# Four of the long-convolution filters' pieces move ahead of the first block's attention

## The chip, the core and the metric

The kernel runs on one core of one Trainium2 chip. The metric is the device time of one execution in microseconds (us). The core has a matrix engine (TensorE, PE in the profile, with its weight loads as PEld), a vector engine (VectorE, DVE), an activation engine (ScalarE, ACT), a general engine (GpSimd, POOL) and SyncE (SP), whose queue issues most of the transfers.

## The reference, cut to what matters

Two kinds of layers follow each other, two of each; the change stands in the first kind (`first_block`), so it acts twice. A layer of it takes x of 512 positions by 1024 channels and computes, in float32:

```
h = rms_norm(x, pre_norm[l])
q, k, v, z_a, u_h, z_h, g_a, g_h = split(h @ w_in[l])
o = diff_attention(q, k, v, lam, rel_bias)       # 4 heads, 4 blocks of 128 queries
y_a = rms_norm(o, subln[l]) * (1 - lam_init) * silu(z_a)
filt = hyena_filters(...)                        # needs no x at all
z = fft_long_conv(hv, filt[:, 0], ...) * hx1
z = fft_long_conv(z, filt[:, 1], ...) * hx2
y_h = z * silu(z_h)
x = x + rms_norm((sigmoid(g_a) * (y_a @ w_pa) + sigmoid(g_h) * (y_h @ w_ph)) @ w_out)
```

`hyena_filters` is a small network of three sine layers over 512 positions, then one product with `w_out` for 2 directions, 2 orders and 512 channels, a decay `exp(-t * |delta|)`, and a transform to frequencies. Attention has two softmaxes for each head; the second is subtracted, scaled by `lam`.

## The kernel before

Large products are made of three float32r matmuls each (`mm3`, L258 to L260), on weights and activations split into a high and a low part (`split`: L266 makes the high part on ACT, L267 the low part on DVE, or on POOL for every third weight chunk). A projection of 128 columns takes 24 such matmuls of 512 columns (`projT`), on one weight chunk that is loaded (L280) and split first.

`layer1` opens the filters as a generator, `filters(l)`, and runs it in pieces, each to its next `yield`. Three pieces are the sine layers (matmul L467; the vector chain L469 to L478; the sine L479). After them come four groups, one for each of 2 orders and 2 halves of the channels, and a group has six pieces:

- four pieces t = 0 to 3, each with four matmuls (L503, L504) on the sines' result `a3` (L482, L483), the decay's exponent on ACT (L508 to L511), the product with it on DVE (L512), and a sum and a difference on POOL (L514, L515). Pieces 0 and 1 split their result (L266, L267), piece 3 makes two more combinations on POOL (L522, L524) and splits both. The first of the four also loads and splits the group's weights (L492, L493, L266, L267 as `fwh` and `fwl`) and its `deltas` (L496, L497).
- two pieces of transform, with twelve matmuls each (`mm3` in `bank`), DVE work L542 to L554, POOL L555, and in the second piece four stores to DRAM (L556, L557).

The pieces use tiles of tag `f`, of which there are eight in turn, and two banks of accumulators that are the filters' alone in this stage (`fl`, `ft`).

Three pieces run before the values' projection. The other 24 are drawn inside `attention1`, one or two ahead of each block of queries:

```
NX, ZS, FS = (1, 1, 1, 0), (3, 3, 7, 11, 13, 14, 15), (2, 1, 2, 1)
for _ in proj(-1):            # keys and queries of head 0
    pass
for hd in range(4):
    for i in range(4):
        for _ in range(FS[i]):
            next(flt, None)   # pieces of the filters
        # scores L667, L668; bias and maximum L671; L675
        # exponentials L677; L680 to L684; next(nxt): projections
```

`FS` says how many pieces go ahead of blocks 0 to 3 of a head, `NX` how many steps of the next head's projections go behind a block, `ZS` when the convolution's own projections (`hyena_v`) are drawn. The bias of a head has one buffer, loaded at the head's start (L449).

This is the order of the program. The order on each engine is another: the kernel is built in `tile.TileContext(nc, schedule_with_timeline_sim=True)`, so a planner with a time model puts the instructions into each engine's list, taking at each moment, among those whose inputs it believes ready, the one that stands earliest in the program. On the chip each engine then works its list in that order.

Of the kernel before, what the change touches and what calls it, by code (L numbers as in the profile page):

```python
# [168 lines left out]
class Kern:  # L169
# [390 lines left out]
    def attention1(self, l, h, v, flt, zv):  # L560
# [31 lines left out]
        def proj(hd):  # L592

            if hd < 3:
                ps = self.ps("acc")
                self.projT(self.wchunk(A[f"win{l}"][5 + hd], 8, P), h, ps)

                ka, kb = (self.T("qk", dt=F32R) for _ in range(2))
                la, lb = rest[hd % 2]
                nc.scalar.activation(ka[a], ps[a], AF.Copy)  # L600
                nc.scalar.activation(kb[b], ps[b], AF.Copy)
                nc.vector.tensor_tensor(la[a], ps[a], ka[a].bitcast(F32), op=SUB)
                nc.vector.tensor_tensor(lb[b], ps[b], kb[b].bitcast(F32), op=SUB)
                nc.gpsimd.tensor_copy(ka[b], ka[a])
                nc.gpsimd.tensor_copy(kb[a], kb[b])
                yield
                ps = self.ps("acc")
                self.projT(self.wchunk(A[f"win{l}"][1 + hd], 8, P), h, ps)

                qa, qb = (self.T("qk", dt=F32R) for _ in range(2))  # L610
                nc.scalar.activation(qa[a], ps[a], AF.Copy, scale=0.125)
                nc.scalar.activation(qb[b], ps[b], AF.Copy, scale=0.125)
                stt(qa[b], ps[a], 0.125, qa[a].bitcast(F32), op0=MUL, op1=SUB)
                stt(qb[a], ps[b], 0.125, qb[b].bitcast(F32), op0=MUL, op1=SUB)
                qk[hd + 1] = (qa, ka, la), (qb, kb, lb)
                yield
            if hd >= 0:
                ps = self.ps("acc")
                self.projT(self.wchunk(A[f"win{l}"][12 + hd], 8, P), h, ps)
                gate[hd] = self.T("o")  # L620
                self.silu2(gate[hd], ps)
# [25 lines left out]
            nc.gpsimd.memset(la[b].bitcast(F32), 0.0)  # L647
            nc.gpsimd.memset(lb[a].bitcast(F32), 0.0)

        NX, ZS, FS = (1, 1, 1, 0), (3, 3, 7, 11, 13, 14, 15), (2, 1, 2, 1)  # L650
        for _ in proj(-1):
            pass
        for hd in range(4):
# [199 lines left out]
    def layer1(self, l, h):  # L853
        nc, A = self.nc, self.A
        self.c1 = self.cq.tile([P, C1_N], F32, tag=f"c1{l}", name=f"c1{l}")
        nc.sync.dma_start(self.c1, A[f"c1{l}"])

        with self.stage(f"a{l}", dict(v=1, p=4, wt=2, o=4)):
            with self.stage(f"q{l}", dict(qk=8, ql=2, bias=1)), self.stage(f"f{l}", dict(f=8, fw1=1, fw23=1, fb=1, a3=1, fd=1, fwh=1, fwl=1)):

                self.fx = self.X((P, 4, S), F32R)
                flt = self.filters(l)
                self.apart = True
                for _ in range(3):
                    next(flt)
                v = self.T("v", (P, 4, S))
                self.projN(v, [A[f"wv{l}"][kc] for kc in range(4)], h, S)
                if l == 0:
                    self.bias_table()
                ma = []  # L870
                ya = self.attention1(l, h, v, flt, self.hyena_v(l, h, ma))
                assert next(flt, 0) == 0
                self.apart = False
        if "ya" in self.dbg:
            self.dump(ya, "ya")
        with self.stage(f"b{l}", dict(mg=1)):
            mg = []
            with self.stage(f"h{l}", dict(Y=4, iv=1, hx=2, gz=1, e=2, y=1)), \
                    self.stage(f"i{l}", dict(sd=2, sds=1, qd=4, hs=4, w=4, ab=2)):
                z = self.hyena(l, h, self.gates(l, h, ma, mg))  # L880
            self.mix1(l, h, ya, z, ma, mg)
# [778 lines left out]
```

## Time and profile before

| | |
|---|---|
| three runs | 1885.38, 1890.8, 1893.59 us; median 1890.8 |
| profiled execution, its own time | 1893.08 us |
| its span, first to last instruction | 1891.3 us |
| mean granted TensorE clock | 0.992 of full |
| PE busy | 98% of the span |
| DVE, ACT, POOL busy | 66%, 48%, 35% |

A matmul's end in the profile is modelled, so a busy PE may still be waiting a little; idle time of an engine that sets no end costs nothing. The attention of the first layer of this kind lies at about 60 to 218 us of the span, that of the second at about 514 to 668 us.

### The profile page before, as it was taken

How to read it: one execution, taken by the hardware profiler on the slowest of the kernel's cores; microseconds unless marked ns; L12 is line 12 of the kernel's file. 1: busy time of each engine (PE TensorE's matmuls, PEld its weight loads, DVE VectorE, ACT ScalarE, POOL GpSimd, SP SyncE). 2: the span in 40 equal slices, each digit the busy share in tenths (PEclk: the TensorE clock that was granted, in tenths of full speed). 3: DMA queues.
4: the chain of work that ended last, by engine and by line, in shares of the span. 5: the costliest groups of instructions: out<-in, count | busy, mean ns of one | idle time of the engine just before them, and what ended most of it. 6: DMA issues, size and time to landing. Idle time of an engine off the chain costs nothing.

```text
span 1891.3 us, 26054 instructions
## 1 busy us (share of the span) xinstructions
PE 1854.0 (98%) x9604; PEld 1560.9 (83%) x9604; DVE 1254.6 (66%) x2238; ACT 900.1 (48%) x1761; POOL 659.9 (35%) x566
## 2 busy tenths in 40 slices
PE   8999999999999999999999999999999999999998
PEld 5878888887788788888888888888888888888886
DVE  6898688664788849775567954757235895465722
ACT  4766432334476542223455356656325535665631
POOL 2455343443245535443146332111114643311110
PEclk9999999999999999999999989999999998999999
DMA  5333433324323353233332321213343222121242
GB/s 178 98 120 110 145 112 107 112 89 164 116 96 106 105 160 108 100 101 123 128 105 70 97 73 30 69 59 115 101 136 101 79 84 79 36 69 59 77 131 90
DMA packets 75656, 190.84 MB, mean 101 GB/s; under 512 B 15714, under 2 KB 25698, under 8 KB 75528
## 3 DMA queue, kind: packets, MB, share of 16 engines
q1 hardware_dynamic: 69448, 184.71, 30.1%
q0 software_dynamic: 1696, 3.41, 0.7%
q10 hardware_dynamic: 4384, 1.05, 0.3%
q8 instruction: 76, 1.25, 0.3%
q14 instruction: 52, 0.43, 0.1%
HBM read 171.29 MB, written 17.84 MB: 100 GB/s over the span
## 4 chain that ended last, share of the span: by engine, by line
PE 75%; DVE 13%; issue 4%; ACT 3%; POOL 3%; DMA 2%; ACTq 0%; SPq 0%; DVEq 0%; POOLq 0%
PE acc L258 13%; PE acc L260 13%; PE acc L259 13%; PE fl L259 5%; PE fl L258 5%; PE fl L260 5%; PE av L1181 2%; DVE wl L267 2%; DVE g L1005 1%; PE av L259 1%; PE av L258 1%; PE av L260 1%; PE av L588 1%; PE lg L259 1%; PE lg L260 1%
## 5 line engine op out<-in xcount | busy, mean ns | idle before, releaser
L266 ACT ACTIVATE wh<-wr 128x1024 fp32r<-128x1024 f32 (+3 forms) x268 | 256.0, 955 | 448.3 <-PE acc L259 160.9
L258 PE MATMUL acc<-u,wh 128*128 128x512 f32 x996 | 397.1, 399 | 0.2
L259 PE MATMUL acc<-u,wh 128*128 128x512 f32 x996 | 393.2, 395 | 0.0
L260 PE MATMUL acc<-u,wl 128*128 128x512 f32 x996 | 392.5, 394 | 0.0
L267 POOL TENSOR_TENSOR wl<-wr,wh 128x1024 fp32r<-128x1024 f32 (+3 forms) x86 | 186.2, 2165 | 490.1 <-ACT wh L266 451.0
L267 DVE TENSOR_TENSOR wl<-wr,wh 128x1024 fp32r<-128x1024 f32 (+3 forms) x182 | 217.5, 1195 | 170.0 <-ACT wh L266 159.6
L258 PEld LDWEIGHTS acc<-u,wh 128*128 128x128 f32 x996 | 187.2, 188 | 42.7 <-issue 3.7
L260 PEld LDWEIGHTS acc<-u,wl 128*128 128x128 f32 x996 | 187.2, 188 | 39.5 <-issue 2.6
L259 PEld LDWEIGHTS acc<-u,wh 128*128 128x128 f32 x996 | 187.3, 188 | 38.3 <-issue 2.9
L259 PE MATMUL fl<-u,wh 128*128 128x512 f32 x316 | 128.6, 407 | 0.0
L260 PE MATMUL fl<-u,wl 128*128 128x512 f32 x316 | 126.5, 400 | 0.0
L258 PE MATMUL fl<-u,wh 128*128 128x512 f32 x316 | 125.9, 398 | 0.0
L260 PE MATMUL acc<-wh,u 128*128 128x512 f32 (+1 forms) x212 | 79.5, 375 | 0.3
L258 PE MATMUL acc<-wh,u 128*128 128x512 f32 (+1 forms) x212 | 78.2, 376 | 1.6 <-DVE l L702 1.2
L259 PE MATMUL acc<-wl,u 128*128 128x512 f32 (+1 forms) x212 | 78.7, 371 | 0.0
L260 PEld LDWEIGHTS fl<-u,wl 128*128 128x128 f32 x316 | 60.3, 191 | 14.9 <-issue 3.0
L259 PEld LDWEIGHTS fl<-u,wh 128*128 128x128 f32 x316 | 60.3, 191 | 13.3 <-issue 2.0
L258 PEld LDWEIGHTS fl<-u,wh 128*128 128x128 f32 x316 | 60.1, 190 | 13.2 <-issue 1.5
L677 ACT ACTIVATE p<-p,mx 128x512 f32<-128x512 f32 x64 | 45.7, 715 | 37.4 <-DVE mx L675 37.4
L790 POOL TENSOR_TENSOR w<-w,ab 128x256 f32<-128x256 f32 x32 | 37.7, 1179 | 69.2 <-DVE w L789 64.0
L321 ACT ACTIVATE sq<-x 128x512 f32<-128x512 f32 x40 | 25.2, 631 | 68.6 <-DVE x L1613 38.2
L1168 ACT ACTIVATE p<-p,amx 128x128 f32<-128x128 f32 (+1 forms) x64 | 35.8, 560 | 28.2 <-DVE amx L1167 27.5
(636 smaller groups left out, 4438.7 us busy)
## 6 DMA issues: line engine op xcount, KB each, us to landing
wr<-in_win SPq DMA_DIRECT2D x88, 512.0 KB, 3.5
wr<-in_xin SPq DMA_DIRECT2D x64, 512.0 KB, 3.4
wr<-in_xout SPq DMA_DIRECT2D x32, 512.0 KB, 3.5
hd<-f SPq DMA_DIRECT2D x32, 256.0 KB, 4.2
hs<-hd SPq DMA_DIRECT2D x32, 256.0 KB, 2.8
wr<-in_wout SPq DMA_DIRECT2D x16, 512.0 KB, 3.4
xd<-x SPq DMA_DIRECT2D x12, 512.0 KB, 3.1
x<-xd SPq DMA_DIRECT2D x12, 512.0 KB, 4.8
```

Source lines behind the costliest of these rows:

```text
L258: mm(ps, l[0], r[0], start=first, stop=False)
L259: mm(ps, l[0], r[1], start=False, stop=False)
L260: return mm(ps, l[1], r[0], start=False, stop=last)
L266: nc.scalar.activation(hi, src, AF.Copy)
L267: (nc.gpsimd if pool else nc.vector).tensor_tensor(lo, src, hi.bitcast(F32), op=SUB)
L321: self.nc.scalar.activation(self.T("sq"), self.xt(i)[:, h * S:(h + 1) * S], AF.Square, scale=1.0 / math.sqrt(D), accum_out=self.ms2[i][:, ...
L588: nc.tensor.matmul(po[:, i], wt[:, kt], v[:, kt, hd * P:(hd + 1) * P], start=kt == 0, stop=kt == 3)
L677: nc.scalar.activation(pp[c], pp[c], AF.Exp, bias=mx[:, c:c + 1], accum_out=s0[:, i:i + 1] if c == 0 else s)
L790: nc.gpsimd.tensor_tensor(a[:, 0], a[:, 0], b[:, 1], op=ADD)
L1005: nc.vector.scalar_tensor_tensor(y[:, d:], ps[:, :S - d], w(n), y[:, d:], op0=MUL, op1=ADD)
L1168: nc.scalar.activation(p[:, :n], p[:, :n], AF.Exp, bias=mx, scale=scale, accum_out=s)
L1181: mm(po[:, ts], v[hd // 4][:, k, (hd % 4) * P:(hd % 4 + 1) * P], w[:, k], start=k == 0, stop=k == i)
```

## The change

Four pieces are drawn between the values' projection (and, in the first layer, the bias table) and the attention; `FS` is lowered by one, so that 5 pieces stand beside each of the four heads and the sum stays 4 + 4 x 5 = 24. No instruction is added or taken away.

```
-        NX, ZS, FS = (1, 1, 1, 0), (3, 3, 7, 11, 13, 14, 15), (2, 1, 2, 1)
+        NX, ZS, FS = (1, 1, 1, 0), (3, 3, 7, 11, 13, 14, 15), (2, 1, 1, 1)
...
                 self.projN(v, [A[f"wv{l}"][kc] for kc in range(4)], h, S)
                 if l == 0:
                     self.bias_table()
+                for _ in range(4):
+                    next(flt)
                 ma = []
                 ya = self.attention1(l, h, v, flt, self.hyena_v(l, h, ma))
```

The four are pieces t = 0 to 3 of the first group. Before, a head held just one group; after, each head begins one piece further back in the cycle: head 0 has both transform pieces of group 0 ahead of its block 0 and then t = 0, 1, 2 of group 1, and so on, until head 3 ends on the last transform piece, as before.

## Rows read from the trace of the kernel before

**Rows 1.** The page: span, and busy time of each engine.
```profile
span 1891.3 us, 26054 instructions
...
PE 1854.0 (98%) x9604; PEld 1560.9 (83%) x9604; DVE 1254.6 (66%) x2238; ACT 900.1 (48%) x1761; POOL 659.9 (35%) x566
```

**Rows 2.** The page: the chain that ended last, by engine.
```profile
PE 75%; DVE 13%; issue 4%; ACT 3%; POOL 3%; DMA 2%; ACTq 0%; SPq 0%; DVEq 0%; POOLq 0%
```

**Rows 3.** Windows: stretch, length; busy PE, PEld, DVE, ACT, POOL; clock; DMA.
```profile
60.00:94.00 34.00, 34.00 (x184) 29.27 (x183) 30.48 (x57) 23.70 (x44) 14.60 (x13) 1.00 0.27 85
94.00:130.00 36.00, 34.11 (x181) 27.20 (x180) 32.97 (x57) 22.10 (x48) 20.05 (x17) 1.00 0.33 112
...
168.00:218.00 50.00, 50.00 (x279) 43.18 (x278) 43.89 (x81) 28.64 (x59) 21.87 (x20) 1.00 0.52 168
218.00:240.00 22.00, 22.00 (x111) 18.54 (x110) 5.01 (x8) 8.56 (x18) 4.72 (x3) 1.00 0.29 93
...
584.00:626.00 42.00, 39.88 (x216) 34.19 (x216) 36.73 (x60) 26.00 (x52) 24.01 (x19) 1.00 0.28 89
626.00:668.00 42.00, 39.01 (x226) 33.34 (x225) 32.64 (x68) 26.60 (x58) 23.86 (x19) 1.00 0.40 129
```

**Rows 4.** Waits of PE, 42 to 240 us: total, times, longest.
```profile
PE fl L258 <- DVE f L512: 1.1, 1, 1.1
PE tr L584 <- DVE o L640: 0.4, 1, 0.4
PE fl L503 <- DVE f L512: 0.3, 1, 0.3
PE fl L504 <- DVE fwl L267: 0.3, 1, 0.3
PE ft L503 <- DVE f L512: 0.2, 1, 0.2
```

**Rows 5.** Waits of PE, 500 to 700 us, the longest of them.
```profile
PE lg L667 <- DVE mx L671: 5.1, 3, 2.1
```

**Rows 6.** Timeline of DVE at a head's start in the second layer.
```profile
631.44 0.69 DVE L671 CUSTOM_DVE_ANT_0 p<-lg,bias 128x512 f32<-128x512 f32 x1 [1.52 <-DMA bias<-db]
```

**Rows 7.** Timeline of DVE: third sine's start and `a3`'s end, both layers.
```profile
52.36 0.80 DVE L469 TENSOR_SCALAR f<-ft,fb 64x512 f32<-64x512 f32 x1 [0.73 <-PE ft L467]
...
60.27 0.68 DVE L483 TENSOR_TENSOR a<-f,a 64x512 fp32r<-64x512 f32 x1 [0.81 <-ACT a L482]
...
513.61 0.80 DVE L469 TENSOR_SCALAR f<-fl,fb 64x512 f32<-64x512 f32 x1 [0.75 <-PE fl L467]
...
530.36 0.69 DVE L483 TENSOR_TENSOR a<-f,a 64x512 fp32r<-64x512 f32 x1
```

**Rows 8.** Timeline of PE: first score and first piece, in both layers.
```profile
60.12 0.39 PE L667 MATMUL lg<-qk,qk 128*128 128x512 f32 x1
...
65.11 0.28 PE L503 MATMUL fl<-fwh,a 128*128 128x256 f32 x1
...
514.30 0.39 PE L667 MATMUL lg<-qk,qk 128*128 128x512 f32 x1
...
531.72 0.28 PE L503 MATMUL ft<-fwh,a 128*128 128x256 f32 x1
```

**Rows 9.** Timeline of SP's queue: load of the first group's weights.
```profile
50.74 0.58 SPq L492 DMA_DIRECT2D f<-in_fwo  x1
```

**Rows 10.** Groups by line and form, DVE, 60 to 240 us.
```profile
L267 DVE TENSOR_TENSOR u<-f,u 128x512 fp32r<-128x512 f32 x16 | 12.3, 778 | 0.7 <-ACT u L266 0.7
...
L512 DVE TENSOR_TENSOR f<-fl,f 128x512 f32<-128x512 f32 x8 | 5.5, 685 | 0.1
...
L267 DVE TENSOR_TENSOR fwl<-f,fwh 128x512 fp32r<-128x512 f32 x3 | 3.1, 1041 | 0.1
```

**Rows 11.** Timeline of POOL and of DVE around 77 us.
```profile
76.99 1.30 POOL L522 TENSOR_TENSOR f<-x 128x512 f32<-128x512 f32 x1
...
77.09 1.74 DVE L684 SCALAR_TENSOR_TENSOR p<-p,cc,p 128x512 f32<-128x512 f32 x1
```

More of the change, by code (lines that the diff above doesn't have):

```diff
@@ L648, in attention1 @@
             nc.gpsimd.memset(lb[a].bitcast(F32), 0.0)
-        NX, ZS, FS = (1, 1, 1, 0), (3, 3, 7, 11, 13, 14, 15), (2, 1, 2, 1)
+        NX, ZS, FS = (1, 1, 1, 0), (3, 3, 7, 11, 13, 14, 15), (2, 1, 1, 1)
         for _ in proj(-1):
@@ L869, in layer1 @@
                     self.bias_table()
+                for _ in range(4):
+                    next(flt)
                 ma = []
```

## The prediction

> **What bounds the kernel now.** I read the page first: PE is busy for 98% of a span of 1891.3 us, DVE for 66%, the others for less [rows 1]. The chain that ended last is 75% PE and 13% DVE [rows 2]. So time is won only where PE stands still, and lost only where it is made to. The question is where PE stands still in the two stretches of attention, since the change moves work only there. The windows say it by head [rows 3]: in the first layer PE is busy for all of 34.00 us of head 0 and all of 50.00 us of head 3, and short by 36.00 - 34.11 = 1.9 us in head 1; in the second layer it is short by 2.1 us in 584 to 626 and by 3.0 in 626 to 668. DVE is close behind in the same stretches: 30.48 of 34, 32.97 of 36, 36.73 of 42 [rows 3]. The granted clock is 1.00 in all of them, the upper of its two levels (2.4 GHz), so no stretch has a slow clock to win back.
>
> Then PE's own waits. In the first layer they sum to 1.1 + 0.4 + 0.3 + 0.3 + 0.2 = 2.3 us, and 1.9 of these are waits for pieces of the filters (L512, and `fwl`) [rows 4]. In the second layer nearly all is one kind: a score (L667) that waits until DVE has taken the scores before it out of their bank (L671), 5.1 us in three waits [rows 5]. One of the three is not DVE's load: DVE itself stood for 1.52 us until the head's bias had landed in its one buffer [rows 6]. That leaves at least 5.1 - 1.5 = 3.6 us that come from DVE's being late. What the change could take away is thus 1.9 + 3.6 = 5.5 us, and all of PE's waits here are 2.3 + 5.1 = 7.4 us.
>
> **The change, part by part.** No instruction is added or removed: the 24 pieces, their loads and their stores all stay, so busy time on every engine stays, and what counts is when.
>
> *When the four can start.* In the program they now stand ahead of head 0's keys and queries, but they need `a3`, the last step of the third sine. In the first layer `a3` is ready at 60.27 + 0.68 = 60.95 us, in the second at 530.36 + 0.69 = 531.05 [rows 7]. The first scores start at 60.12 and at 514.30, the first piece's matmul at 65.11 and at 531.72 [rows 8]. This is the point of the argument: pieces 0 and 1 stood ahead of block 0's scores in the program before as well, and yet PE ran scores first, by 5.0 us in one layer and by 17.4 in the other. Readiness placed them, not the program. Moved up further, they still can't start before `a3`: 60.95 against 65.11 leaves at most 4.2 us, 531.05 against 531.72 leaves 0.7. The sines aren't moved. So the four pieces do not go into the projection ahead of attention, where DVE has room; they go closer together at the start of head 0, and pieces 2 and 3 go ahead of the softmax of blocks 1 and 2.
>
> *Their loads.* The first group's weights are loaded at 50.74 us [rows 9], 10 us before `a3`; earlier than that is worth nothing. Their place on SP's queue moves past the loads for keys and queries of head 0 and the bias. Should the load stand before one of those and wait for its `f` tile, the weight chunks behind it would be late; I cost this at nothing, since two chunks are loaded ahead and PE's 34.00 of 34.00 shows none late [rows 3]. If that cover were gone, a late chunk would cost up to the 1.5 us that the late bias cost DVE [rows 6].
>
> *What heads gain.* The four pieces are four products at 685 ns, four low parts at 778 and one `fwl` at 1041 on DVE [rows 10]: 4 x 0.685 + 4 x 0.778 + 1.04 = 6.9 us in a layer. A head held one whole group; heads 1 to 3 now hold a piece less, on the average 6.9 / 4 = 1.7 us of DVE less beside 36 to 50 us. That is the relief: from 92% of a head to about 87% (32.97 - 1.7 of 36). The waits worth 5.5 us are those where DVE is a little late, by 2.1 us at most [rows 5], so a relief of that size should remove some. Ends: nothing, if the planner fills the room with other work; all 5.5, if each wait is of that kind. I take about half, 3 us: the relief is as large as a typical wait, but it doesn't fall on the very block that is late.
>
> *What head 0 pays.* Four pieces follow each other at `a3`, on two banks, and then both transform pieces stand ahead of block 0 in the program. Ends: nothing, since head 0 lost nothing with three pieces in its first two blocks (34.00 of 34.00); or, in each layer, the 1.9 us that head 1 of the first layer loses with a group beside it [rows 3], 3.8 in all. I take 1 us, nearer to head 0's row, since it is the same head, and PE has other projections in reach there. What covers the delay of block 0's softmax is those projections; at the end of attention PE is still full, 22.00 of 22.00 with DVE at 5.01 [rows 3], so the store of such work does not run out.
>
> *Sum.* -3 + 1 = -2 us. The profiled execution took 1893.08 us, its span and 1.8 around it, so 1893.1 - 2 = 1891.1; it lies 2.3 above the runs' median of 1890.8, so on the median's scale 1888.8, say 1889. The bounds of the two terms, -5.5 and +3.8, give 1885 to 1895.
>
> **The rivals.**
>
> *Slower: PE waits in its list.* PE works its list in order. If the planner, believing `a3` earlier than it is, puts the first piece's matmul directly behind head 0's queries, PE stands until `a3`. In the first layer that is from 60.12 to 61.6 (`a3` and the 0.7 us that lay between it and L503 in the second layer), 1.5 us. In the second it is from 514.30: if the third sine then took the first layer's 8.6 us (52.36 to 60.95 [rows 7]), `a3` would be ready at 522.2, and PE would stand for 8.6 us; with its present 17.4 us, for 17. Together 10 to 19 us: 1901 to 1910. It decides from a place about 9 us too early in the second layer. For it: 531.72 is only 0.7 us behind `a3`, so the list there has no slack. Against it: the planner already had these pieces ahead in the program and did not do it. Chance 0.12.
>
> *Slower: POOL's sums hold DVE.* Beside a sum on POOL of 1.30 us (L522) a DVE product that started 0.10 us later took 1.74 us [rows 11]; its own end came 0.54 us after POOL's. The four pieces have ten such sums in a layer; if each came to hold the softmax's DVE work of head 0 by as much as 1.3 us, that is 13 us of DVE in a layer, and if half of it in both layers reached PE, 13 us: 1904. Against it: the same sums hold DVE somewhere today. Chance 0.06. The Trainium skill has the rule, on its page "SBUF — State Buffer", section "SBUF: two separate sides": VectorE and GpSimd have one pair of ports in common, and whoever starts first keeps it for its whole instruction. The trace agrees with that here, the 1.74 us above.
>
> *Faster: DVE paces the heads.* With DVE at 92% of head 1, the heads might shrink by all of DVE's relief: 6.9 us in each layer, 13.8 in all, 1877. Against it: the four pieces stay in head 0 by `a3`, and all of PE's waits in both stretches are 7.4 us; more than that can come only from later stages whose order falls better. Chance 0.18.
>
> *Nothing moves.* The lists come out nearly as before, since readiness rules: 1891. Chance 0.14.
>
> **How the numbers follow.** My forecast has 0.50. A measurement of this kernel tells about 0.5% from no change, 9.5 us: 1881.3 to 1900.3. Forecast and "nothing moves", 0.64, lie within. The faster rival, and a few cases of the forecast in which later stages gain too, make 0.20; the two slower ones, less the mildest of them, 0.16. The range reaches from 1878, which takes in most of the way to the faster rival's 1877, to 1902, which takes in the near end of the first slower one; the likeliest case alone is 1885 to 1895.
>
> **What would show it.** Right: the first L503 still starts behind the first scores and within some us of `a3`; L503 of pieces 2 and 3 closer behind, transform matmuls beside block 0 or 1; windows of heads 1 to 3 with DVE busy lower by some 1.7 us each, and PE's waits for L671 and L512 down from 7 to about 4 us. Wrong: a PE wait of several us at L503 just behind the first scores; `a3` itself ready earlier (the sines moved after all); or a difference that arises outside both stretches of attention.

## The result, and the profile after

The changed kernel is slower: median 1904.14 us of 8 runs (1898.87 to 1910.95) against 1890.89 us of 8 runs of the kernel before (1881.45 to 1894.87), ratio 1.0074, 95% interval 1.0054 to 1.0095. The forecast was 1889 us, its range 1878 to 1902. The profiled execution took 1898.87 us, the shortest of the eight. Its page, span, busy time and the chain that ended last, which answer to [rows 1, 2]:

```profile
span 1897.1 us, 26030 instructions
...
PE 1852.9 (98%) x9604; PEld 1561.6 (82%) x9604; DVE 1249.7 (66%) x2238; ACT 899.0 (47%) x1761; POOL 659.0 (35%) x566
...
PE 66%; DVE 15%; issue 3%; ACT 2%; POOL 2%; DMA 2%; ACTq 0%; SPq 0%; DVEq 0%; POOLq 0%
```

The work is the same to a few us, and each engine's count of instructions is the same; PE's part of the chain fell from 75% to 66%. The windows say in which heads (columns as in [rows 3]; the second layer now runs some 9 us later, so its two stretches are shifted by that):

```profile
60.00:94.00 34.00, 34.00 (x184) 29.24 (x183) 30.01 (x57) 23.43 (x44) 14.58 (x13) 1.00 0.27 85
94.00:130.00 36.00, 33.61 (x178) 28.59 (x178) 31.77 (x63) 24.54 (x53) 20.63 (x18) 0.95 0.36 123
168.00:218.00 50.00, 46.38 (x240) 39.05 (x239) 39.09 (x78) 23.92 (x50) 19.78 (x18) 0.93 0.46 148
...
593.00:635.00 42.00, 42.00 (x230) 36.16 (x229) 35.98 (x59) 26.43 (x55) 23.02 (x18) 1.00 0.33 111
635.00:677.00 42.00, 38.48 (x203) 31.77 (x202) 32.77 (x64) 24.11 (x53) 21.81 (x19) 1.00 0.46 153
```

Head 0 is untouched. Head 1 of the first layer is short by 2.4 us of PE where it was short by 1.9, and head 3 by 3.6 where it was full; both now run at a granted clock of 0.95 and 0.93, which was 1.00. That alone is 36 x 0.05 + 50 x 0.07 = 5.3 us. In the second layer the loss lies ahead of these stretches, as the short windows show; 569 to 581 us there is the end of head 1 and the start of head 2:

```profile
97.00:104.00 7.00, 5.23 (x22) 4.04 (x20) 5.45 (x12) 6.38 (x20) 3.19 (x3) 0.76 0.39 130
183.00:191.00 8.00, 4.38 (x22) 2.97 (x21) 7.93 (x12) 5.11 (x15) 4.47 (x5) 0.85 0.37 121
569.00:581.00 12.00, 7.83 (x40) 5.76 (x38) 11.43 (x21) 8.53 (x15) 7.16 (x7) 0.86 0.30 106
```

In the kernel before PE was all but full in the same places, at 1.00:

```profile
97.00:104.00 7.00, 6.88 (x38) 5.54 (x37) 6.92 (x12) 5.06 (x10) 4.12 (x4) 1.00 0.37 143
183.00:191.00 8.00, 8.00 (x43) 6.80 (x43) 7.43 (x17) 6.23 (x19) 6.52 (x8) 1.00 0.00 0
559.00:571.00 12.00, 12.00 (x60) 9.93 (x59) 10.76 (x21) 7.41 (x15) 3.92 (x3) 1.00 0.41 144
```

PE's waits in the changed kernel, first layer (42 to 240 us, to be held against [rows 4]), then second layer (500 to 715 us, against [rows 5]):

```profile
PE lg L667 <- DVE mx L671: 2.0, 1, 2.0
PE fl L503 <- ACT fwh L266: 1.6, 1, 1.6
PE ft L258 <- DVE f L543: 0.9, 1, 0.9
PE av L588 <- ACT wt L586: 0.8, 1, 0.8
PE acc L258 <- DVE x L603: 0.8, 1, 0.8
...
PE tr L584 <- DVE o L640: 2.2, 1, 2.2
PE ft L258 <- ACT u L266: 1.4, 1, 1.4
PE fl L258 <- DVE f L512: 0.9, 1, 0.9
```

The waits are spread over engines and lines: no one of them stands out, and PE's list has nothing at these places that would bridge them. By the end of the second attention (the last L640: 691.33 us before, 706.14 after) 14.8 us are lost, about what the medians differ by, 13.2. That the profiled spans differ by only 5.8 comes from what follows: from the last L827 to the end the same 5442 instructions of PE took 1050.6 us before, at a mean granted clock of 0.99, and 1039.9 after, at 1.00. So a place on the scale of one profile is good to several us only, and the medians decide.

**Why the list is empty there.** I counted, in the traces, the projections' matmuls (L258 to L260 into `acc`, 24 to a projection) that PE has issued since block 0's scores when it comes to the scores of blocks 5 to 8:

```
                   block 5   block 6   block 7   block 8
layer 1, before       96       120       144       168
layer 1, after        96        96       120       168
layer 2, before       96       120       144       168
layer 2, after        96        96       120       120
```

After the change block 6 follows block 5 with no projection between them, and in the second layer block 8 follows block 7 so too. The timeline of PE shows what the first is like:

```profile
96.98 0.39 PE L668 MATMUL lg<-ql,qk 128*128 128x512 f32 x1
99.01 0.39 PE L503 MATMUL fl<-fwh,a 128*128 128x256 f32 x1 [1.64 <-ACT fwh L266]
...
103.47 0.40 PE L668 MATMUL lg<-ql,qk 128*128 128x512 f32 x1
104.62 0.47 PE L258 MATMUL acc<-u,wh 128*128 128x512 f32 x1 [0.75 <-DVE x L603]
```

In the kernel before, ACT waits for the same weights (`fwh`, 4.59 us idle behind the load of `fwo`), and PE works off a projection meanwhile. A projection needs one of the two banks `acc`. One bank is free only when the result in it has been read; the projection at 104.62 waits for just that, the last reading (L603) of the one before it. The other bank would do, but it holds a result that is not read: the convolution's first projection (`hyena_v`, its result leaves through L708 on ACT and L709, L710 on DVE). Its L708 on ACT, before, in the first and in the second layer, with the wait for `fwh` in the first:

```profile
89.29 0.76 ACT L708 ACTIVATE u<-acc,c 128x512 f32<-128x512 f32 x1
...
97.16 0.63 ACT L266 ACTIVATE fwh<-f 128x512 fp32r<-128x512 f32 x1 [4.59 <-DMA f<-in_fwo]
...
107.20 0.63 ACT L266 ACTIVATE u<-f 128x512 fp32r<-128x512 f32 x1 [0.29 <-POOL f L515]
...
542.85 0.77 ACT L708 ACTIVATE u<-acc,c 128x512 f32<-128x512 f32 x1
```

And after, in the first and in the second layer:

```profile
106.84 0.63 ACT L266 ACTIVATE u<-f 128x512 fp32r<-128x512 f32 x1 [0.26 <-POOL f L515]
107.38 0.77 ACT L708 ACTIVATE u<-acc,c 128x512 f32<-128x512 f32 x1
...
575.88 0.63 ACT L266 ACTIVATE u<-f 128x512 fp32r<-128x512 f32 x1 [1.22 <-POOL f L515]
576.54 0.78 ACT L708 ACTIVATE u<-acc,c 128x512 f32<-128x512 f32 x1
```

L708 comes 18 us later in the first layer (34 in the second, 9 of them the shift), though its matmuls in the first end just ahead of block 4's scores, before 86 us in both kernels, and each time it stands directly behind the first split (L266) of the filters' second group. The two have one thing in common: z, where L708 writes, and that group's split tiles `gh`, `gl` are all tiles of tag `u`, of which the kernel has ten (`pools(10, ...)`). Before, z's projection is drawn behind block 3 and the group's first piece ahead of block 4. After, that piece is drawn ahead of block 1, so it stands first in the program. That is theory D, here still a theory: buffers of one tag are handed out in program order, z waits for a piece that is itself waiting for its weights, and one of two banks is held from 86 to 112 us, when L710 has read it.

### The profile page after: what moved, and what is told of

The parts are those of the page before. It is cut to its first block, busy times and chain, and to the rows that moved or that the text cites. A ratio compares the mean times of both kernels' runs of the same rounds, so it can differ in the third digit from the quotient of the medians.

```text
span 1897.1 us, 26030 instructions
## 1 busy us (share of the span) xinstructions
PE 1852.9 (98%) x9604; PEld 1561.6 (82%) x9604; DVE 1249.7 (66%) x2238; ACT 899.0 (47%) x1761; POOL 659.0 (35%) x566
## 4 chain that ended last, share of the span: by engine, by line
PE 66%; DVE 15%; issue 3%; ACT 2%; POOL 2%; DMA 2%; ACTq 0%; SPq 0%; DVEq 0%; POOLq 0%
PE acc L260 11%; PE acc L258 11%; PE acc L259 11%; PE fl L258 5%; PE fl L259 5%; PE fl L260 5%; DVE wl L267 2%; PE av L1183 2%; DVE g L1007 2%; DVE st L1395 1%; DVE u L1397 1%; PE av L258 1%; PE av L259 1%; PE av L260 1%; PE av L818 1%
## 5 line engine op out<-in xcount | busy, mean ns | idle before, releaser
L266 ACT ACTIVATE wh<-wr 128x1024 fp32r<-128x1024 f32 (+3 forms) x268 | 256.0, 955 | 462.9 <-PE acc L259 175.8
L258 PE MATMUL acc<-u,wh 128*128 128x512 f32 x996 | 398.0, 400 | 1.1 <-DVE x L603 1.0
L260 PE MATMUL acc<-u,wl 128*128 128x512 f32 x996 | 393.0, 395 | 0.0
L267 POOL TENSOR_TENSOR wl<-wr,wh 128x1024 fp32r<-128x1024 f32 (+3 forms) x86 | 185.2, 2153 | 485.7 <-ACT wh L266 432.6
L267 DVE TENSOR_TENSOR wl<-wr,wh 128x1024 fp32r<-128x1024 f32 (+3 forms) x182 | 215.9, 1187 | 174.3 <-ACT wh L266 170.7
L258 PEld LDWEIGHTS acc<-u,wh 128*128 128x128 f32 x996 | 187.9, 189 | 43.5 <-issue 3.5
L260 PEld LDWEIGHTS acc<-u,wl 128*128 128x128 f32 x996 | 187.8, 189 | 39.6 <-issue 2.6
L258 PE MATMUL fl<-u,wh 128*128 128x512 f32 x316 | 124.8, 395 | 0.0
L260 PE MATMUL fl<-u,wl 128*128 128x512 f32 x316 | 124.7, 395 | 0.0
L260 PE MATMUL acc<-wh,u 128*128 128x512 f32 (+1 forms) x212 | 79.5, 375 | 0.3
L258 PE MATMUL acc<-wh,u 128*128 128x512 f32 (+1 forms) x212 | 77.8, 375 | 0.4 <-ACT u L266 0.2
L260 PEld LDWEIGHTS fl<-u,wl 128*128 128x128 f32 x316 | 59.5, 188 | 13.9 <-issue 2.2
L258 PEld LDWEIGHTS fl<-u,wh 128*128 128x128 f32 x316 | 59.5, 188 | 12.5 <-issue 0.9
```

Of the source, the lines that this page charges most:

```text
L258: mm(ps, l[0], r[0], start=first, stop=False)
L260: return mm(ps, l[1], r[0], start=False, stop=last)
L266: nc.scalar.activation(hi, src, AF.Copy)
L267: (nc.gpsimd if pool else nc.vector).tensor_tensor(lo, src, hi.bitcast(F32), op=SUB)
```

## The experiments

Ratios are to the kernel before, with the 95% interval. The last column of the table is the start of the last L827 (the end of the second layer's convolution) in each profile, less the 840.7 us of the kernel before. It is a landmark of one execution each: the last row, whose ratio is 1.0003, has +4.5, so differences of that size mean nothing there.

```
run                                      ratio  interval           L827
the change                              1.0074  1.0054 to 1.0095  +16.5
early four, heads as before             1.0009  0.9987 to 1.0030   +2.0
five per head, no early four            1.0085  1.0054 to 1.0117  +14.3
change in the first layer only          1.0047  1.0024 to 1.0069   +6.2
change in the second layer only         1.0027  1.0009 to 1.0045   +5.1
one piece ahead of the convolution      1.0037  1.0013 to 1.0061   +7.0
change, z with a buffer of its own      1.0298  1.0268 to 1.0328   +4.5
before, z with a buffer of its own      1.0282  1.0254 to 1.0310   -0.4
change, convolution drawn earlier       1.0024  1.0005 to 1.0043   +3.8
change, z written to early              1.0014  0.9993 to 1.0035   +3.9
change, weights with a tile of their own 1.0084 1.0053 to 1.0116  +15.4
before, weights with a tile of their own 1.0003 0.9984 to 1.0022   +4.5
```

**Which half of the change.** The first two runs each do one half of it.

```
-        NX, ZS, FS = (1, 1, 1, 0), (3, 3, 7, 11, 13, 14, 15), (2, 1, 2, 1)
+        NX, ZS = (1, 1, 1, 0), (3, 3, 7, 11, 13, 14, 15)
+        FS = ((0, 0, 1, 1),) + 3 * ((2, 1, 2, 1),)
...
-                for _ in range(FS[i]):
+                for _ in range(FS[hd][i]):
...
+                for _ in range(4):
+                    next(flt)
```

> The four pieces stand ahead of the attention as in the changed kernel, but heads 1 to 3 draw six each in the places they had before (head 0 draws its last two beside its scores). Theory A (the early place does nothing, the five per head in heads 1 to 3 cost): 1891 us, ratio 0.998 to 1.002, and the TensorE waits of both attentions as in the kernel before (8.9 us above the pitch in the first). Rival B (the early place itself costs): about 1904 us, ratio 1.005 to 1.009. Rival C (half each): ratio about 1.0035.

```
+        FS = ((6, 1, 1, 1),) + 3 * ((2, 1, 1, 1),)
```

> No piece stands ahead of the attention (head 0 draws nine of its own beside its scores), heads 1 to 3 draw five as in the changed kernel. Theory A: the order that the planner gives is the changed kernel's and so is the time, 1904 us, ratio 1.005 to 1.009, with the same TensorE waits at the second head and the same drops of the granted clock behind them. Rival B (the early place costs): 1891 us, ratio 0.998 to 1.002. Rival C (half each): ratio about 1.0035.

Measured 1.0009 and 1.0085. The new place of the four pieces costs nothing that the interval can tell; that heads 1 to 3 draw five, and head 0 therefore three more of the second group, costs as much as the whole change.

**Which layer.**

```
+        FS = (2, 1, 1, 1) if l == 0 else (2, 1, 2, 1)
...
+                for _ in range(4 if l == 0 else 0):
+                    next(flt)
```

> The change in the first layer alone. Theory A (stalls that the list of each layer makes): the first attention ends some 6 us later than before, the second layer runs as before: 1897 us, ratio 1.002 to 1.005. Rival (the clock's chance, or one place of the second layer): ratio 0.999 to 1.001.

The other run has `l == 1` in both places.

> The change in the second layer alone. Theory A: the first layer as before, the second attention about 5 us longer (14.8 us of the changed kernel's landmarks at its end less the 9.3 that the first layer brings): 1897 us, ratio 1.002 to 1.005; with the run before, the two parts add up to the whole, 1.007. Rival (all of it comes in the first layer and is carried on): ratio 0.999 to 1.001.

1.0047 and 1.0027; that they add up to just the 1.0074 of the whole is closer than their intervals warrant, but each lies clear of 1. It is something that the list of each layer makes anew, and no single accident.

**One piece.** The kernel before, with only the first piece of the second group drawn ahead of block 3 and not of block 4:

```
+        FS = ((2, 1, 2, 2), (1, 1, 2, 1)) + 2 * ((2, 1, 2, 1),)
```

> The kernel before with one piece moved by one block: the first piece of the second group is drawn ahead of block 3 and not of block 4, and so ahead of the convolution's first projection; every other count is that of before from block 5 on. Theory D (buffers of tag u are handed out in program order, so the convolution's first result, L708, waits for that group's first split, L266, and holds one of the two banks acc meanwhile): as the changed kernel, ratio 1.005 to 1.009, with L708 directly behind the split at about 107 us. Rival E (five pieces per head in heads 1 to 3 shift the phase of all that follows, whatever the buffers): 23 of 24 pieces stand as before, ratio 0.999 to 1.002.

1.0037: one piece of 24, moved by one block, gives half of the loss, and in either layer the same counts of projections ahead of blocks 5 to 8 as the change (96, 96, 120, 168 and 96, 96, 120, 120). The size expected was twice that, so the other pieces' places count as well; but the rival's 1.000 lies outside the interval (the upper end of what it expected, 1.002, does not), and it has no reason for L708's new place. In the first layer the trace shows where it loses less: in 168 to 218 us PE is busy for 48.26 us at a clock of 0.97, in the changed kernel for 46.38 at 0.93. ACT's timeline in this run (L709 is the L708 of before):

```profile
106.16 0.61 ACT L266 ACTIVATE u<-f 128x512 fp32r<-128x512 f32 x1
106.68 0.76 ACT L709 ACTIVATE u<-acc,c 128x512 f32<-128x512 f32 x1
```

**z without the common buffers.** Change and control:

```
             self.up = e(tp(name="u", bufs=nu, reuse_waits="tile"))
+            self.zp = e(tp(name="z", bufs=1, reuse_waits="tile"))
...
-        self.z = z = self.U()
+        self.z = z = self.zp.tile([P, 4, S], F32, tag="z", name=self.nm("z"))
...
-        with k.pools(10, dict(acc=2, fl=1, lg=2, tr=1, ft=1, av=1)):
+        with k.pools(9, dict(acc=2, fl=1, lg=2, tr=1, ft=1, av=1)):
```

> The change in full, but the convolution's input z has a buffer of its own and tag u has nine and not ten, so the memory is the same. Theory D: L708 comes at about 89 us again, the projections ahead of block 6 are 120 again, and the loss goes: ratio 0.997 to 1.002; what is then left is what the prediction meant by relief (2 us or 0.1% faster). Rival E: ratio 1.005 to 1.009 as the change.

> The control: the kernel before with the same separate buffer for z. Both theories: ratio 0.998 to 1.002. If nine buffers in the other stages cost or bring something, it shows here and is to be taken off the run with the change.

With z apart, L708 (L709 in this kernel) comes at 89.04 us, and the projections' matmuls ahead of blocks 6 to 8 are 120, 144 and 168 in both layers, as expected. The control was needed more than I thought: with nine buffers the kernel loses some 50 us behind the last L827, the largest wait behind 745 us being

```profile
PE av L1229 <- POOL lu L1240: 16.7, 2, 8.4
```

which the kernel before has not. Both ratios missed what was expected of them. Against each other, change to control, the medians 1945.37 and 1942.84 us give 1.0013 (their two ratios 1.0016; six runs each): with z apart, the change costs about a fifth of what it costs with the common buffers. The price of nine buffers is so much larger than the effect that I did not rest on this alone.

**z written to early.** All ten buffers, the change in full, and one small instruction:

```
-        NX, ZS, FS = (1, 1, 1, 0), (3, 3, 7, 11, 13, 14, 15), (2, 1, 1, 1)
+        NX, ZS, FS = (1, 1, 1, 0), (0, 3, 7, 11, 13, 14, 15), (2, 1, 1, 1)
...
         self.z = z = self.U()
+        self.nc.gpsimd.memset(z[:, :, 0:1], 0.0)
         yield
```

> The change in full, ten buffers of tag u as before, and one instruction more in each layer: z is opened behind block 0 and one column of each of its four rows is written at once on POOL (overwritten later), so that z gets its buffer ahead of the second group's first piece, which is drawn ahead of block 1. Theory D (order of buffers): L708 comes at about 89 us again, projections ahead of block 6 are 120, and ratio 0.999 to 1.003, the 1.0016 of the two runs with a separate buffer in the middle. Rival E (five per head alone): ratio 1.005 to 1.009. If it came out under 0.998, the relief that the prediction counted on is there.

1.0014, with 1 inside the interval: an instruction added takes the loss away, or all but about a fifth of it. ACT's timeline, and the windows where PE stood still:

```profile
89.74 0.76 ACT L708 ACTIVATE u<-acc,c 128x512 f32<-128x512 f32 x1
...
107.42 0.63 ACT L266 ACTIVATE u<-f 128x512 fp32r<-128x512 f32 x1 [0.29 <-POOL f L515]
```

```profile
97.00:104.00 7.00, 7.00 (x40) 6.06 (x39) 5.99 (x12) 4.83 (x10) 4.87 (x4) 1.00 0.39 150
183.00:191.00 8.00, 6.01 (x26) 5.02 (x27) 7.69 (x16) 5.28 (x19) 5.79 (x6) 0.79 0.22 67
564.00:576.00 12.00, 12.00 (x60) 9.92 (x59) 10.76 (x21) 7.41 (x15) 3.93 (x3) 1.00 0.41 144
```

L708 is back, and in both layers the projections' matmuls ahead of blocks 6, 7 and 8 are 120, 144 and 168 again. PE still waits 1.6 us for DVE (L667 for L671) in the second of these windows; that may be the rest. Whether opening z early without writing to it would do was not tried on the chip.

**The convolution drawn earlier.** No instruction added:

```
+        NX, ZS, FS = (1, 1, 1, 0), (0, 0, 7, 11, 13, 14, 15), (2, 1, 1, 1)
```

> The change in full, but the convolution's buffer is opened and its first projection drawn behind block 0 and not behind block 3, so ahead of the second group's first piece again; buffers as they were. Theory D: ratio 0.997 to 1.003, L708 ahead of the split. Rival E: ratio 1.005 to 1.009.

1.0024, most of it back but not all. The trace shows two new waits. One is the same thing at another place: the gates' first result (L834, it too writes to a `u`) now stands behind a split of the filters, and PE waits 2.6 us for its bank. The other is what the prediction's first rival had described: in the second layer the first L503 stands in PE's list ahead of other work and waits 2.5 us for `a3` (L483).

```profile
192.18 0.65 ACT L266 ACTIVATE u<-f 128x512 fp32r<-128x512 f32 x1
192.69 0.61 ACT L834 ACTIVATE u<-acc 128x512 f32<-128x512 f32 x1
```

```profile
PE acc L258 <- ACT u L834: 2.6, 1, 2.6
...
PE ft L503 <- DVE a L483: 2.5, 1, 2.5
```

**Is it the weights' load?** The wait of L503 for `fwh` is the first that one sees after the change, so I took it away, in the change and in the kernel before:

```
-                wraw, wh, wl = self.T("f", (P, 2, 256)), self.T("fwh", (P, 2, 256), F32R), self.T("fwl", (P, 2, 256), F32R)
+                wraw, wh, wl = self.T("fr", (P, 2, 256)), self.T("fwh", (P, 2, 256), F32R), self.T("fwl", (P, 2, 256), F32R)
...
-            with self.stage(f"q{l}", dict(qk=8, ql=2, bias=1)), self.stage(f"f{l}", dict(f=8, fw1=1, fw23=1, fb=1, a3=1, fd=1, fwh=1, fwl=1)):
+            with self.stage(f"q{l}", dict(qk=8, ql=2, bias=1)), self.stage(f"f{l}", dict(f=7, fr=1, fw1=1, fw23=1, fb=1, a3=1, fd=1, fwh=1, fwl=1)):
```

> The change in full, but the filters' weights have a tile of their own (one of the eight f), so their load need not wait for an f. Rival F (it is ACT's wait for the weights, fwh behind the load, that leaves TensorE without work): the wait of L503 for fwh goes and with it the loss, ratio 0.998 to 1.002. Theory D: L708 still stands behind the second group's first split, which comes earlier by some us, and block 6 still has 96 projections ahead of it, so part of the loss stays: ratio 1.003 to 1.008.

> The kernel before with the same own tile for the weights (seven f and not eight). A control for the run with the change, and an attempt at a faster kernel: ACT stands 4.6 us for that load in the first layer. Theory D: that idle time is covered by projections, so ratio 0.998 to 1.002. Rival F: it costs something today, ratio 0.996 to 0.999.

1.0084 and 1.0003. The wait for `fwh` is gone from PE's waits, and the time is not; L708 still comes after the split (102.95 and 101.19 us), and block 6 still has 96 matmuls of projections ahead of it in both layers. The wait that one sees first was not the cause. No version here is faster than the kernel before.

## Why the prediction was wrong

*When the four can start*: right. `a3`'s last step (L483) and the first piece's matmul behind it stand as worked out, in either layer:

```profile
60.71 0.69 DVE L483 TENSOR_TENSOR a<-f,a 64x512 fp32r<-64x512 f32 x1 [0.81 <-ACT a L482]
...
539.68 0.69 DVE L483 TENSOR_TENSOR a<-f,a 64x512 fp32r<-64x512 f32 x1
```

```profile
65.55 0.28 PE L503 MATMUL fl<-fwh,a 128*128 128x256 f32 x1
...
541.03 0.28 PE L503 MATMUL ft<-fwh,a 128*128 128x256 f32 x1
```

The gaps are 4.2 and 0.7 us as in [rows 7, 8]; the half of the change that is only this measures 1.0009.

*Their loads* and *what head 0 pays*: no loss in head 0 of the first layer, 34.00 of 34.00, so the +1 us was 0 there, and the profile shows no wait of PE in that of the second. The error does not lie here.

*What heads gain*: this is the step that failed. "Heads 1 to 3 now hold a piece less" was true, and DVE does less beside them: in 94 to 130 us of the first layer 31.77 us where it was 32.97, 1.2 us less (1.7 had been worked out; the window is fixed, the heads run later, so this is a rough measure). But the step took the twenty other pieces as merely fewer in each head. A piece less in heads 1 to 3 is three pieces more ahead of them: the second group's first three went from head 1's blocks into head 0's, past the draw of the convolution's first projection behind block 3. I had checked what the four early pieces move past and never asked it of the others; the sum has no term for it. The rule that I leaned on, readiness and not program order places an instruction, holds for data; for the buffers of one tag, program order decided when z could be written. In place of -2 us the runs show +13.2: from this order some +11 (1.0074 less the 1.0014 that is left when z is written early), and a rest of 0.14% that its interval, 0.9993 to 1.0035, does not tell from nothing.

The -3 us did not come either. In the run that writes z early, heads 1 to 3 hold five pieces and the order of the buffers is that of before, so the relief should show: the ratio's lower end, 0.9993, leaves room for a gain of 1.3 us and not for one of 2. PE's waits for L671 in the second layer fell from 5.1 to 3.7 us, but in the first a new one of 1.6 us came up; all of PE's waits in both layers sum to 8.1 us there and to 7.6 in the kernel before. So the relief removed some waits, and others came up at other blocks.

About half of the loss is the lower clock. The mean granted clock is 0.9888 over the eight runs of the change and 0.9927 over the 30 runs of the kernel before beside the first four experiments: 0.0039 of 1891 us are 7 of the 13 us (an estimate). In the twelve runs that write z early it is 0.9929. The profiled execution agrees: 5.3 us in the first attention (from the windows above), 5 x 0.34 = 1.7 between the two (0.66 in 454 to 459 us) and 12 x 0.14 = 1.7 in the second; the rest of the 14.8 us is PE standing still, whose waits in the two attentions sum to 13.8 us where they were 7.6. The prediction had the clock at 1.00 in these stretches [rows 3] and gave it no term.

The rivals. *PE waits in its list* has the sign and by chance the size, but not the place: the first L503 stands as far behind the first scores as before, 5.0 us in the first layer. *POOL's sums hold DVE* gives 1904 too, and is not it: the run that writes to z early has all these sums in the same pieces, and sums that hold DVE longer would show in its busy time, which went from 1254.6 to 1249.7 us. It has a share in one stall, though. Beside a sum (L524, 1.73 us from 184.66) a split of the weights on DVE (L267) took 2.29 us where the ones at 91 and 101 us took 1.22 and 1.26, and the L671 that PE's wait of 2.0 us was for stands right behind it in DVE's list:

```profile
185.18 2.29 DVE L267 TENSOR_TENSOR wl<-wr,wh 128x1024 fp32r<-128x1024 f32 x1
187.40 0.68 DVE L671 CUSTOM_DVE_ANT_0 p<-lg,bias 128x512 f32<-128x512 f32 x1
```

So the rule that the Trainium skill gives on its page "SBUF — State Buffer", section "SBUF: two separate sides", agrees with this trace too; it does not decide the whole, since the kernel before has such places as well [rows 11]. *DVE paces the heads* and *nothing moves* are out. None of the five cases had the mechanism.

What is open: that buffers are handed out in the order of the program is what the runs on z and the place of L708 in each bear out; how the planner does it was not seen, and whether a tile's opening or its first write counts, these runs do not separate. That the held bank is what thins the projections is read from the counts and from the wait for L603; a third bank was not tried. How the rest of 0.14% arises, if there is one, and why one piece moved gives half and not all, was not tried.

## What to carry to other kernels

When generators are drawn a step earlier, list for every tag which tiles are first written between the old and the new place of every piece, the shifted ones too: a tile whose first write falls behind another's may wait for it (here L708 behind the split), and with it the accumulator bank that it was to empty. Look at what drains a bank (here L708, 18 us late) before the waits that PE shows: they were many different ones, and taking the first away brought nothing. If a buffer's turn must be kept, a tiny early write to it keeps it, at no price that these runs can tell from nothing.

## What had not been expected of the hardware

The granted clock fell where PE had stood still for a couple of us: 0.76 over 97 to 104 us, 0.85 and 0.86 over the stretches that hold waits of 2.0 and 2.2 us, so that part of each ran at 1.2 GHz and not at 2.4. The same stretches of the kernel before, without these waits, show 1.00, and so do the first and third of them in the run that writes to z early; the second, where it still waits 1.6 us, shows 0.79. In the changed kernel these three falls cost 7 x 0.24 = 1.7, 8 x 0.43 = 3.4 (0.57 over 188 to 196 us) and 1.7 us, beside waits of 2.4, 3.6 and 3.6 us in the same places: from half of the waiting to nearly all of it. It is no fixed price. The kernel before has a wait of 2.1 us in 584 to 626 at 1.00 [rows 3, 5], and the run that writes to z early shows 0.95 over 94 to 130 us, where its longest waits are 0.9 and 0.6 us.
